# Attention output projection of a hybrid decoder step: when the shares of the merge are loaded and accumulated

## The chip, the cores and the metric

The kernel runs on one core of one Trainium2 chip. The metric is device time in microseconds (us) of one execution. Five engines work beside each other, each on its own list of instructions in a fixed order: TensorE (PE, with its weight loads as PEld), VectorE (DVE), ScalarE (ACT), GpSimd (POOL) and SyncE (SP). SP issues nearly all loads; POOL issues the transfers that add to what lies in SBUF ("accumulating" below). All transfers are carried by the core's 16 DMA engines.

## The reference, cut to what matters

One layer of a decoder for 1024 prompt tokens and 8 sample tokens (1032 columns, `TT`), width 1024. Three branches read the same normalised input, and their outputs are gated, summed and projected:

```python
y_c = jnp.einsum('bhlm,bmhd->blhd', probs, mem_v).reshape(bsz, seq, ATTN_DIM) @ w_attn_o
g_a, g_b, g_c = jnp.split(jax.nn.sigmoid(gates), N_BRANCHES, axis=-1)
merged = g_a * y_a + g_b * y_b + g_c * y_c
return merged @ w_merge_o, (sc_new, ssm_conv_new, ssm_new)
```

A SwiGLU block and a final norm follow. All is float32 in and out. A product is made of three passes over operands that are split into a high and a low part (high x high, high x low, low x high).

## The kernel before, in words

Activations lie as eight tiles of 128 partitions x 1032 columns, features on the partitions. The columns are handled in two halves of 516 (`HS`); the eight sample tokens are the last eight columns of the second half.

The first two branches are ready early: `g_a*y_a` lies in DRAM as `mg_d[m]`, `g_b*y_b` as `yg_d[m]`, for the eight output tiles m. These two are called the *shares* of tile m. The third branch is made last: the attention output of the prompt is loaded back as `raw8[0..7]` (line 1837), the sample columns are put into it by `s_back` from a PSUM tile (line 1752: four copies on DVE, four on ACT), and `y_c` is the product of `raw8` with `w_attn_o`.

That product is done by a Strassen-like scheme with seven half-size products on 2x2 blocks. The blocks of the activations and their sums and differences are called *forms*: B11, B21, T1, nT2, T3, B22, T4, four pieces each. A form is split into high and low by ACT (line 444) and DVE (line 446). T1 is `b12 - b11` (line 1887) and nT2 is `T1 - b22` (line 1891). Both need the second half of the columns, so their last eight columns need `s_back`. In the kernel before, T1 and nT2 are formed in two pieces each: 508 columns, and then the eight sample columns.

The output tiles are made in four pairs, m = 0, 2, 4, 6, called pair one to four below. Each pair runs `strassen` (line 298 is its matmul, and the names ao0, ao2, ao4, ao6 belong to the pairs): weights `ao{m}r` are loaded in two blocks into a ring of three buffers (line 279), their sums `sa` and `sb` are made on DVE (`sb` ends at line 331), and all are split (lines 285 and 286; `S`, `T`, `A`, `D` name the splits). Within it, `mid` calls `fetch` ahead of the product with T3: it loads the pair's two gates `gt_d[16+m]`, `gt_d[17+m]` (line 1956) and, from pair three on, the shares.

`shares(ms)` loads `yg_d[m]` into a new tile `merged[m]` on SP (line 1930), placed behind the last weight block issued so far (`issue_after(last_raw[0])`), and then has POOL accumulate `mg_d[m]` onto it (line 1931), which waits until the load has landed. Pair two's shares are called for ahead of its `strassen`. For pair one the tile is first filled with the gated product itself, and POOL then accumulates `yg_d` and `mg_d` onto tile 0 and 1 (line 1982, four transfers).

After a pair's product, DVE multiplies with the gates (lines 1970, 1971, 1975) and, for pairs two to four, adds onto `merged` (1973, 1974, 1977). Lines 432 and 434 are subtractions that end the pair's outputs and release PSUM.

All eight merged tiles are split (`mgs0`..`mgs7`, lines 180 and 181) and multiplied with `w_merge_o` (blocks `wm..`, line 170 and 171 for their split, line 2050 for the matmuls), in the order 0 to 7 of the inner index k.

The program's order is only a wish. The order on each engine is worked out ahead of the run by a planner, which takes, engine by engine, what is ready by its own estimate of durations, the earlier written first. `tc.issue_after(x)` adds one rule: the instructions in the block stand behind `x` on the queue of `x`. During the run each engine goes through its list strictly in order and waits where an input is late, whatever stands behind.

Of the kernel before, what the change touches and what calls it, by code (L numbers as in the profile page):

```python
# [12 lines left out]
ALU = mybir.AluOpType  # L13
# [4 lines left out]
P = 128  # L18
D = 1024
T = 1024  # L20
NS = 8
TT = T + NS
NCH = 3
CW = TT // NCH
HT = TT // 2
HC = HT // 2
KD = D // P
# [16 lines left out]
def tile_kernel(ctx: ExitStack, tc, a, o):  # L44
    nc = tc.nc
    V, S, G, PE, SY = nc.vector, nc.scalar, nc.gpsimd, nc.tensor, nc.sync

    def f32(t):
        return t.bitcast(F32)
# [24 lines left out]
    def act_tile(part, name, dt=F32R, shape=(P, TT)):  # L74
        return ap_.tile(list(shape), dt, tag=part, name=name)
# [101 lines left out]
    def split_act(src, name):  # L177
        hi = act_tile("ah", name + "h")
        lo = act_tile("al", name + "l")
        S.copy(hi, src)  # L180
        V.tensor_sub(lo, src, f32(hi))
        return hi, lo
# [74 lines left out]
    HS = [slice(0, HT), slice(HT, TT)]  # L257
# [17 lines left out]
    last_raw = [None]  # L275
# [167 lines left out]
    def split_to(hi, lo, src, behind=None):  # L443
        S.copy(hi, src)
        with nullcontext() if behind is None else tc.issue_after(behind):
            V.tensor_sub(lo, src, f32(hi))
# [6 lines left out]
    gt_d = dram("gt_d", [24, P, TT])  # L453
    mg_d = dram("mg_d", [KD, P, TT])
    yr_d = dram("yr_d", [KD, P, TT])
    yg_d = dram("yg_d", [KD, P, TT])
# [34 lines left out]
    with tc.tile_pool(name="p0", bufs=1) as p0, tc.tile_pool(name="pop", bufs=1, space=PSUM) as pop:  # L491
# [23 lines left out]
        ps = sm_ps("ps_mix")  # L515
# [6 lines left out]
        for key, src, n in (  # L522
# [13 lines left out]
            while done < n:  # L536
                b, off = divmod(at, P)
                m = min(n - done, P - off)
# [1093 lines left out]

    raw8, aforms = [], {}

    def aform(f, kt, src, c=slice(0, HT)):
        if kt % 2 == 0 and c.start == 0:
            mk = afx.get(f) or (lambda part, nm: act_tile(part, nm, shape=(P, 2, HT)))
            pair = [mk(part, f"a{f}{kt}{part}") for part in ("ah", "al")]
            aforms.setdefault(f, []).extend(tuple(t[:, i, :] for t in pair) for i in range(2))
        split_to(*(t[:, c] for t in aforms[f][kt]), src)  # L1640

    afx = {}
    if True:
# [100 lines left out]
        def s_back():  # L1744
            t = ev_tile("osr", (NS, D))
            SY.dma_start(t, os_d)
            ps = sm_ps("psob")
            for i in range(8):
                PE.transpose(ps[:, i * NS : (i + 1) * NS], t[:, i * P : (i + 1) * P], ident[:NS, :NS])
            for kt in range(KD):  # L1750
                cp_ = V.tensor_copy if kt < 4 else S.copy
                cp_(raw8[kt][:, T:TT], ps[:, kt * NS : (kt + 1) * NS])

        heads = {}
        slot = [None]
# [125 lines left out]
        one = lambda n: fxo.tile([P, TT], F32, tag="one", bufs=1, name=n)  # L1881
        begun = []
        ahead_of_last.append(lambda: begun.extend(st_begin(wa[0], wa[1], "ao0", lambda n: one(n)[:, :1024])))
        for c in (slice(0, T - HT), slice(T - HT, HT)):
            for kt in range(4):
                b11, b12 = (raw8[kt][:, h][:, c] for h in HS)
                V.tensor_sub(b11, b12, b11)
                aform("T1", kt, b11, c)
            for kt in range(4):
                t1, b22 = (raw8[kt + 4 * i][:, HS[i]][:, c] for i in range(2))  # L1890
                V.tensor_sub(t1, t1, b22)
                aform("nT2", kt, t1, c)
        run_next(outs)
        owed.pop()()

# [22 lines left out]
    merged = []  # L1918
# [4 lines left out]
        V.tensor_add(sa[:, 512:], sa[:, :512], raw1[:, :512])  # L1923
        return sa, st_split(sa, f"{nm}S")

    def shares(ms):
        for m in ms:
            merged.append(big(f"mg{m}"))
            with tc.issue_after(last_raw[0]):
                SY.dma_start(merged[m], yg_d[m])  # L1930
            G.dma_start(merged[m], mg_d[m], accum_op=ALU.add)

    second = []

    def last_forms_and_second():
        last_aforms()
# [4 lines left out]
    for m in range(0, KD, 2):  # L1941
        gts = []
        if m == 0:
            oo = oos[0]
        elif m == 2:
            oo = oos[1] + [ev_tile("ao21")[:, :TT]]
            begun = second
            shares(range(2, 4))
        else:
            oo = [ev_tile(f"ao{m}{i}")[:, :TT] for i in range(2)]  # L1950
            begun = None

        def fetch():
            for i in range(2):
                gts.append((ev_tile if i else one)(f"gt3{m + i}")[:, :TT])
                SY.dma_start(gts[i], gt_d[16 + m + i])
            if m > 2:
                shares(range(m, m + 2))

        pa = strassen(  # L1960
            wa[m], wa[m + 1], aforms, f"ao{m}", ev_sums, lambda: tuple(t[:, c] for t in oo for c in HS),
            begun=begun, mid=fetch, hook=None if m else form3,
            after_t3=None if m else last_forms_and_second, head=heads_[m // 2] if m < 4 else None,
        )
        if m == 2:
            accs.clear()
            accs.extend((ta, tb, tc_))
        c1, c0 = HS[1], HS[0]
        to = [big(f"mg{i}") for i in range(2)] if m == 0 else oo
        V.tensor_mul(to[0], oo[0], gts[0])  # L1970
        V.tensor_mul(to[1][:, c1], oo[1][:, c1], gts[1][:, c1])
        if m:
            V.tensor_add(merged[m], merged[m], to[0])
            V.tensor_add(merged[m + 1][:, c1], merged[m + 1][:, c1], to[1][:, c1])
        V.scalar_tensor_tensor(to[1][:, c0], pa, -1.0, gts[1][:, c0], op0=ALU.mult, op1=ALU.mult)
        if m:
            V.tensor_add(merged[m + 1][:, c0], merged[m + 1][:, c0], to[1][:, c0])
        else:
            merged += to
            for src in (yg_d, mg_d):  # L1980
                for i in range(2):
                    G.dma_start(merged[i], src[i], accum_op=ALU.add)
    fxo_stack.close()
    aux_stack = ExitStack()
    auxp = aux_stack.enter_context(tc.tile_pool(name="aux", bufs=3))
# [1 line left out]
    def aux(name):  # L1987
        return auxp.tile([P, TT], F32, tag="aux", name=name)

    mg = [split_act(merged[m], f"mgs{m}") for m in range(KD)]  # L1990

    x2 = [None] * KD
    rfs = [None, None]
# [32 lines left out]
    def form_first(kt):  # L2026
        form("B11", kt, normed(kt, 0))
# [4 lines left out]
    for half in range(2):  # L2032
        sq = ev_tile(f"sq{half}")
        for m in range(KD):
            xt = aux(f"xT{half}{m}")
            SY.dma_start(xt[:, :HT], xT_d[m][:, HS[half]])
            wh, wl = weights(wblock(a["w_merge_o"][0], m * P), f"wm{half}{m}")
            if half == 0:
                x2[m] = big(f"x2_{m}")
            t = x2[m][:, HS[half]]  # L2040

            def merge_part(out, ns):
                for k, (ah, al) in enumerate(mg):
                    if k in (0, 3, 6) and ns[0] == 0:
                        tick()
                    ks = slice(k * P, (k + 1) * P)
                    for i, (wt, x) in enumerate(((wh, ah), (wh, al), (wl, ah))):
                        for n, po in zip(ns, out):
                            lo, hi = HALF[n]
                            PE.matmul(  # L2050
                                po, wt[:, ks], x[:, half * HT + lo : half * HT + hi],
                                start=(k == 0 and i == 0), stop=(k == KD - 1 and i == 2),
                            )

            if half == 1 and m == KD - 1:

                for n, (lo, hi) in enumerate(HALF):
                    ps = sm_ps(f"pm{half}{m}{n}")[:, : hi - lo]
                    merge_part([ps], (n,))
                    V.tensor_tensor(t[:, lo:hi], ps, xt[:, lo:hi], op=ALU.add)  # L2060
            else:
                ps = next_ps(f"pm{half}{m}")
                merge_part([hv(ps)[:, lo:hi] for lo, hi in HALF], (0, 1))
                V.tensor_tensor(t, hv(ps), xt[:, :HT], op=ALU.add)  # L2064
            if m == 0:
                S.activation(sq[:, :HT], t, AF.Square)
            else:
                S.activation(xt[:, :HT], t, AF.Square)
                V.tensor_add(sq[:, :HT], sq[:, :HT], xt[:, :HT])
            S.dma_start(x2_d[m][:, HS[half]], t)  # L2070
        if half == 0:
            pend.extend([None, None] + [lambda sq=sq: norm_half(0, sq)] + [None])
            for kt in range(4):
                pend.extend([lambda kt=kt: form_first(kt), None, lambda kt=kt: form_second(kt), None])
        else:
            flush()
            norm_half(1, sq)
# [26 lines left out]
    for kt in range(4):  # L2104
        b12, b11 = normed(kt, 1), x2[kt][:, HS[0]]
# [3 lines left out]
    for kt in range(4):  # L2109
        t1, b22 = x2[kt][:, HS[0]], normed(kt + 4, 1)  # L2110
        V.tensor_sub(t1, t1, b22)
        form("nT2", kt, t1)
    for kt in range(4):
        b12, b22 = x2[kt][:, HS[1]], x2[kt + 4][:, HS[1]]
# [119 lines left out]
    for part, js in enumerate(([0], [9, 10])):  # L2234
# [9 lines left out]
        for m in range(KD):  # L2244
            if not part:
                x2[m] = big(f"x3_{m}")
            for half in range(2):
                ps = next_ps(f"pd{part}{m}{half}")
                for k, (ah, al) in enumerate(hl):
                    ks = slice(k * cols + m * P % cols, k * cols + m * P % cols + P)  # L2250
# [4 lines left out]
                t = x2[m][:, HS[half]]  # L2255
# [127 lines left out]
    for n3, (c0, c1, tiles) in enumerate(  # L2383
# [3 lines left out]
        for ms in ((0, 1), (2, 3, 4), (5, 6, 7)) if n3 == 0 else ((0, 1, 2), (3, 4, 5), (6, 7)):  # L2387
# [53 lines left out]
```

## Time and profile before

| | |
|---|---|
| median of 3 runs | 2442.67 us (2442.17 to 2443.28) |
| profiled execution, its own time | 2437.72 us |
| its span, first to last instruction | 2436.0 us |
| PE busy | 2392.2 us, 98% of the span |
| DVE busy | 1646.8 us, 68% |
| ACT busy | 1113.5 us, 46% |
| POOL busy | 114.6 us, 5% |
| mean granted TensorE clock | 0.997 |
| moved by DMA | 407.90 MB, mean 167 GB/s |
| queue of SP | 336.44 MB, 44.6% of the 16 engines' span |
| queue of POOL | 5.28 MB, 1.1% |

The attention projection lies between about 1552 us and 1652 us of the span; the merge begins at 1652.10 us. A row of the timeline gives start, duration, engine, line, operation, output tile <- inputs and count; in brackets, how long the engine sat idle just before and what ended that. A row of the waits gives who waited for whom, the total in us, how many times, and the longest. A row of the windows gives a stretch, its length, the busy time of each engine with the number of instructions, the granted clock, the share of the DMA engines and GB/s. Buffer numbers are left out of tile names: `mg` is any of the merged tiles, `ao4r` either weight block of pair three.

### The profile page before, as it was taken

To read this page: it belongs to the slowest core of one execution; us is meant where nothing else is said; L and a number is where in the kernel's file an instruction comes from. 1 tells how busy PE (TensorE), PEld (TensorE's weight loads), DVE (VectorE), ACT (ScalarE), POOL (GpSimd) and SP (SyncE) were. 2 spreads that over 40 slices of the span, in tenths; PEclk is the share of its full clock that TensorE was granted. 3 is DMA by queue.
4 is the path that set the end of the run, shared out by engine and by line. 5 is a ranking of instruction groups with operands and counts; after the bars stand their busy time and mean duration, and the time that the engine had idled before them with its cause. 6 is when DMAs were issued, how large, how long until landed. Compare 5 with 4: busy or idle time off the path is not lost.

```text
span 2436.0 us, 45644 instructions
## 1 busy us (share of the span) xinstructions
PE 2392.2 (98%) x18860; PEld 2284.5 (94%) x18860; DVE 1646.8 (68%) x2689; ACT 1113.5 (46%) x1792; POOL 114.6 (5%) x173
## 2 busy tenths in 40 slices
PE   8999999999999999999999999889999999999998
PEld 6999999999999999888888987889999999999998
DVE  6744677777777775568687764765777655567965
ACT  6643555455454543656555442333553333343423
POOL 0000000000000000212211000010000000000000
PEclk9999999999999999999999999999999999999999
DMA  6444423444444345668787797495455333354622
GB/s 204 135 154 160 137 87 109 136 140 131 125 150 122 115 118 187 215 222 281 247 294 219 272 320 263 142 244 186 141 179 168 101 109 100 97 175 156 192 86 81
DMA packets 356678, 407.90 MB, mean 167 GB/s; under 512 B 15230, under 2 KB 276462, under 8 KB 356463
## 3 DMA queue, kind: packets, MB, share of 16 engines
q1 hardware_dynamic: 331894, 336.44, 44.6%
q10 hardware_dynamic: 23137, 63.26, 6.8%
q0 software_dynamic: 1440, 5.28, 1.1%
q8 instruction: 148, 2.42, 0.4%
q14 instruction: 59, 0.48, 0.1%
HBM read 288.81 MB, written 116.35 MB: 166 GB/s over the span
## 4 chain that ended last, share of the span: by engine, by line
PE 87%; DMA 5%; DVE 4%; issue 2%; ACT 2%; SPq 0%; POOL 0%; DVEq 0%; ACTq 0%; POOLq 0%
PE po L221 7%; PE pm L2050 4%; PE ps_q L221 3%; PE py L1114 1%; PE pss L1127 1%; PE ps_z L221 1%; PE po L1106 1%; DMA in<-yb_d 1%; PE G16m L298 1%; PE d00m L298 1%; PE G22m L298 1%; PE Z2m L298 1%; PE Z14m L298 1%; PE Z6m L298 1%; PE Z8m L298 1%
## 5 line engine op out<-in xcount | busy, mean ns | idle before, releaser
L1058 ACT ACTIVATE r<-r,acum 128x128 f32<-128x128 f32 x256 | 79.3, 391 | 2.8 <-DMA r<-ac_d 1.9
L847 DVE SCALAR_TENSOR_TENSOR ax<-u,prm,ax 128x1024 f32<-128x1024 f32 x44 | 56.4, 1282 | 0.0
L999 ACT ACTIVATE st<-st,es 128x128 f32<-128x128 f32 x128 | 41.3, 392 | 18.2 <-DMA st<-in_state_ssm_dram 15.1
L1091 POOL TENSOR_TENSOR xdd<-xdt,decst 128x512 f32<-128x512 f32 x32 | 35.2, 1101 | 285.3 <-DVE xdt L1087 279.4
L1085 DVE TENSOR_TENSOR r<-r,cbm 128x1024 f32<-128x1024 f32 x32 | 39.2, 1224 | 4.3 <-ACT r L1060 2.4
L1001 DVE SCALAR_TENSOR_TENSOR st<-sr,dts,st 128x128 f32<-128x128 f32 x128 | 40.8, 353 | 0.4
L1110 DVE TENSOR_TENSOR y<-po,ea 128x512 f32<-128x512 f32 x28 | 19.3, 690 | 31.2 <-PE po L1106 31.2
L1005 DVE SCALAR_TENSOR_TENSOR sr<-st,sr 128x128 f32<-128x128 f32 x128 | 35.9, 291 | 1.1
L1127 PE MATMUL pss<-xdd,bT 128*128 128x512 f32 x64 | 34.4, 619 | 2.2 <-ACT bT L1084 1.4
L1114 PE MATMUL py<-r,xdt 128*64 128x128 f32 x512 | 35.0, 279 | 0.0
L1060 ACT ACTIVATE r<-r 128x1024 f32<-128x1024 f32 x32 | 33.8, 1057 | 0.7
L1140 POOL TENSOR_TENSOR s<-s,cdec 128x512 f32<-128x512 f32 x28 | 33.1, 1183 | 0.6 <-DVE s L1133 0.4
L2064 DVE TENSOR_TENSOR x<-pm,xT 128x516 f32<-128x516 f32 x15 | 10.4, 695 | 32.0 <-PE pm L2050 32.0
L1114 PEld LDWEIGHTS py<-r,xdt 128*64 128x64 f32 x512 | 27.3, 136 | 4.4 <-issue 1.0
L1106 PE MATMUL po<-bc,s 128*128 128x128 f32 x224 | 29.5, 275 | 0.0
L1106 PEld LDWEIGHTS po<-bc,s 128*128 128x128 f32 x224 | 28.0, 191 | 1.0
L1694 ACT ACTIVATE pr<-psa,mx 128x256 f32<-128x256 f32 x32 | 14.9, 471 | 30.5 <-DVE mx L1692 26.6
L850 DVE SCALAR_TENSOR_TENSOR ax<-u,prm,ax 128x1032 f32<-128x1032 f32 x22 | 28.4, 1291 | 0.0
L844 ACT ACTIVATE ax<-u,prm 128x1024 f32<-128x1024 f32 x22 | 27.4, 1246 | 1.2 <-ACT u L926 0.4
L1087 DVE TENSOR_TENSOR xdt<-xp,dtT 128x512 f32<-128x512 f32 x32 | 21.9, 685 | 8.8 <-PE xp L1080 8.7
L1084 ACT COPY bT<-bp 128x128 f32<-128x128 f32 x32 | 8.4, 262 | 39.3 <-DVE cbm L1082 39.2
L1682 DVE SCALAR_TENSOR_TENSOR kc<-kc,qb 128x256 f32<-128x256 f32 x64 | 23.8, 421 | 3.3 <-DMA qb<-qs_d 3.3
(9293 smaller groups left out, 9067.4 us busy)
## 6 DMA issues: line engine op xcount, KB each, us to landing
r<-ac_d SPq DMA_DIRECT2D x32, 512.0 KB
gt_d<-G ACTq DMA_DIRECT2D x24, 516.0 KB
gt<-gt_d SPq DMA_DIRECT2D x24, 516.0 KB
xs_d<-ax ACTq DMA_DIRECT2D x22, 516.0 KB
zs<-zs_d SPq DMA_DIRECT2D x16, 516.0 KB
yb_d<-x SPq DMA_DIRECT2D x16, 516.0 KB
in<-yb_d SPq DMA_DIRECT2D x16, 516.0 KB
st<-in_state_ssm_dram SPq DMA_DIRECT2D x32, 256.0 KB
```

The costliest lines, as they stand in the source:

```text
L221: PE.matmul(po, wt[:, ks], xc, start=(k == 0 and i == 0), stop=(k == nk - 1 and i == 2))
L298: PE.matmul(po, wt[:, ks], xc, start=(start and kt == 0 and i == 0), stop=(kt == 3 and i == 2), skip_group_check=True,)
L847: V.scalar_tensor_tensor(acc[:, :T], u[:, j : j + T], w[j], acc[:, :T], op0=ALU.mult, op1=ALU.add)
L999: S.activation(st[:, i], st[:, i], AF.Copy, scale=es[:, g * 4 + i, b : b + 1])
L1001: V.scalar_tensor_tensor(st[:, i], rb, dts[:, g * 4 + i, b : b + 1], st[:, i], op0=ALU.mult, op1=ALU.add)
L1005: V.scalar_tensor_tensor(rb, st[:, i], 1.0, rc, op0=ALU.mult, op1=ALU.mult, accum_out=ys[:, g * 4 + i, b : b + 1],)
L1058: S.activation(r[:, j, :], r[:, j, :], AF.Relu, scale=-1.0, bias=acum[:, c, h : h + 1])
L1085: V.tensor_tensor(r, r, bc(cbm.unsqueeze(1), [P, HPG, P]), op=ALU.mult)
L1106: PE.matmul(po[:, t * P : (t + 1) * P], state["s"][:, t * P : (t + 1) * P], bcg[1][:, cs], start=True, stop=True,)
L1114: PE.matmul(py[hp : hp + 64, (h // 2) * P : (h // 2 + 1) * P], xdt[:, h * 64 : (h + 1) * 64], r[:, (h % 2) * 4 + h // 2, :], start=True, s ...
L1127: PE.matmul(pss, bT, xdd, start=True, stop=True)
L2050: PE.matmul(po, wt[:, ks], x[:, half * HT + lo : half * HT + hi], start=(k == 0 and i == 0), stop=(k == KD - 1 and i == 2),)
```

## The change

Five edits, all around this stage:

1. T1 and nT2 are formed in whole pieces of 516 columns: 8 differences and 8 splits in place of 16 and 16.
2. The copies of the sample columns into `raw8` are all on ACT.
3. The shares of pairs three and four are loaded behind the second gate of the same pair (`got[0]`) instead of behind the last weight block. Pair two's are as before.
4. Pair one's four accumulating transfers are written after pair three's `strassen` and placed behind the last accumulating transfer of pair three (`added[0]`) on POOL's queue.
5. The merge takes its inner index in the order 2, 3, 4, 5, 0, 1, 6, 7, and the merged tiles are split in that order.

```diff
-    def aform(f, kt, src, c=slice(0, HT)):
-        if kt % 2 == 0 and c.start == 0:
+    def aform(f, kt, src):
+        if kt % 2 == 0:
...
-        split_to(*(t[:, c] for t in aforms[f][kt]), src)
+        split_to(*aforms[f][kt], src)
...
-                cp_ = V.tensor_copy if kt < 4 else S.copy
-                cp_(raw8[kt][:, T:TT], ps[:, kt * NS : (kt + 1) * NS])
+                S.copy(raw8[kt][:, T:TT], ps[:, kt * NS : (kt + 1) * NS])
...
-        for c in (slice(0, T - HT), slice(T - HT, HT)):
-            for kt in range(4):
-                b11, b12 = (raw8[kt][:, h][:, c] for h in HS)
-                V.tensor_sub(b11, b12, b11)
-                aform("T1", kt, b11, c)
-            for kt in range(4):
-                t1, b22 = (raw8[kt + 4 * i][:, HS[i]][:, c] for i in range(2))
-                V.tensor_sub(t1, t1, b22)
-                aform("nT2", kt, t1, c)
+        for kt in range(4):
+            b11, b12 = (raw8[kt][:, c] for c in HS)
+            V.tensor_sub(b11, b12, b11)
+            aform("T1", kt, b11)
+        for kt in range(4):
+            t1, b22 = raw8[kt][:, HS[0]], raw8[kt + 4][:, HS[1]]
+            V.tensor_sub(t1, t1, b22)
+            aform("nT2", kt, t1)
...
-    def shares(ms):
+    def shares(ms, behind):
         for m in ms:
             merged.append(big(f"mg{m}"))
-            with tc.issue_after(last_raw[0]):
+            with tc.issue_after(behind):
                 SY.dma_start(merged[m], yg_d[m])
-            G.dma_start(merged[m], mg_d[m], accum_op=ALU.add)
+            added[0] = G.dma_start(merged[m], mg_d[m], accum_op=ALU.add).ins
...
-            shares(range(2, 4))
+            shares(range(2, 4), last_raw[0])
...
-                SY.dma_start(gts[i], gt_d[16 + m + i])
+                got[0] = SY.dma_start(gts[i], gt_d[16 + m + i]).ins
             if m > 2:
-                shares(range(m, m + 2))
+                shares(range(m, m + 2), got[0])
...
+        if m == 4:
+            for src in (yg_d, mg_d):
+                for i in range(2):
+                    with tc.issue_after(added[0]):
+                        G.dma_start(merged[i], src[i], accum_op=ALU.add)
...
             merged += to
-            for src in (yg_d, mg_d):
-                for i in range(2):
-                    G.dma_start(merged[i], src[i], accum_op=ALU.add)
...
-    mg = [split_act(merged[m], f"mgs{m}") for m in range(KD)]
+    mg = [(m, split_act(merged[m], f"mgs{m}")) for m in (2, 3, 4, 5, 0, 1, 6, 7)]
...
-                for k, (ah, al) in enumerate(mg):
+                for k, (kt, (ah, al)) in enumerate(mg):
...
-                    ks = slice(k * P, (k + 1) * P)
+                    ks = slice(kt * P, (kt + 1) * P)
```

More of the change, by code (lines that the diff above doesn't have):

```diff
@@ L1924, in sums_of @@
         return sa, st_split(sa, f"{nm}S")
-    def shares(ms):
+    def shares(ms, behind):
         for m in ms:
             merged.append(big(f"mg{m}"))
-            with tc.issue_after(last_raw[0]):
+            with tc.issue_after(behind):
                 SY.dma_start(merged[m], yg_d[m])
-            G.dma_start(merged[m], mg_d[m], accum_op=ALU.add)
-    second = []
+            added[0] = G.dma_start(merged[m], mg_d[m], accum_op=ALU.add).ins
+    added = [None]
+    second, got = [], [None]
     def last_forms_and_second():
```

## The prediction

> **What bounds the kernel now.** The page comes first: which engine carries the chain that ended last.
>
> ```profile
> span 2436.0 us, 45644 instructions
> PE 87%; DMA 5%; DVE 4%; issue 2%; ACT 2%; SPq 0%; POOL 0%; DVEq 0%; ACTq 0%; POOLq 0%
> ```
>
> PE carries 87%, so an edit pays only where PE stands still for it. The chain of waits between 1590 and 1660 us, the waits from 1480 to 1680 us, and windows of 5 us say where it does.
>
> ```profile
> 1583.75 9.26 issue
> ...
> 1594.66 16.08 DMA mg<-mg_d
> ```
> ```profile
> DVE mg L1974 <- DMA mg<-mg_d: 8.0, 1, 8.0
> ...
> ACT ao4Ah L285 <- DMA ao4r<-in_w_attn_o_dram: 5.5, 1, 5.5
> ...
> PE ao2m L298 <- ACT ao L383: 3.9, 1, 3.9
> ...
> PE ao0m L298 <- ACT aT10ah L444: 1.3, 1, 1.3
> ```
> ```profile
> 1550.00:1555.00 5.00, 5.00 (x43) 4.80 (x41) 5.00 (x13) 1.78 (x3) 0.00 (x0) 1.00 0.51 139
> ...
> 1595.00:1600.00 5.00, 4.01 (x21) 4.01 (x22) 2.61 (x3) 0.94 (x2) 1.56 (x2) 0.68 1.09 322
> ...
> 1615.00:1620.00 5.00, 5.00 (x35) 5.00 (x34) 3.68 (x5) 1.54 (x2) 0.00 (x0) 0.77 1.03 268
> ```
>
> Two stalls stand out. In pair two PE waits 3.9 us for a PSUM copy on ACT that stands behind `ao4Ah`, which waits for a weight block. At pair three DVE waits 8.0 us for an accumulating transfer that took 16.08 us. Afterwards the clock is 0.68 and 0.77 for 5 us. The timeline of POOL shows why that transfer was late.
>
> ```profile
> 1582.73 1.01 POOL L1982 DMA_DIRECT2D mg<-yg_d  x1 [274.03 <-DVE mg L1970]
> 1593.03 0.87 POOL L1982 DMA_DIRECT2D mg<-mg_d  x1 [9.28 <-DMA mg<-yg_d]
> ...
> 1594.12 2.44 POOL L1931 DMA_DIRECT2D mg<-mg_d  x2
> ...
> 1626.06 0.85 POOL L1931 DMA_DIRECT2D mg<-mg_d  x1 [18.03 <-DMA mg<-yg_d]
> 1627.76 0.86 POOL L1931 DMA_DIRECT2D mg<-mg_d  x1 [0.85 <-DMA mg<-yg_d]
> ```
>
> Pair two's two transfers (1594.12) stand behind pair one's, for whose first POOL waits 9.28 us. DVE and PE, each by its timeline:
>
> ```profile
> 1602.11 0.69 DVE L434 TENSOR_TENSOR ao<-ao,ao2m 128x516 f32<-128x516 f32 x1
> 1610.83 0.70 DVE L1974 TENSOR_TENSOR mg<-mg,ao 128x516 f32<-128x516 f32 x1 [8.03 <-DMA mg<-mg_d]
> ...
> 1612.58 1.22 DVE L286 TENSOR_TENSOR ao4Sl<-ao4sa,ao4Sh 128x1024 fp32r<-128x1024 f32 x1
> ...
> 1616.80 0.69 DVE L331 SCALAR_TENSOR_TENSOR ao4sb<-ao4sa,ao4r 128x512 f32<-128x512 f32 x1
> ...
> 1628.10 0.69 DVE L1974 TENSOR_TENSOR mg<-mg,ao 128x516 f32<-128x516 f32 x1
> ...
> 1631.38 1.22 DVE L286 TENSOR_TENSOR ao6Sl<-ao6sa,ao6Sh 128x1024 fp32r<-128x1024 f32 x1
> ```
> ```profile
> 1581.40 0.51 PE L298 MATMUL ao2m<-aT10ah,ao2Sh 128*128 128x256 f32 x2 [3.12 <-ACT ao2Sh L285]
> ...
> 1613.86 0.80 PE L298 MATMUL ao4m<-aT10ah,ao4Sl 128*128 128x256 f32 x2 [5.62 <-DVE ao4Sl L286]
> ...
> 1635.47 0.40 PE L298 MATMUL ao6m<-aT10ah,ao6Sl 128*128 128x256 f32 x2
> ...
> 1656.40 0.41 PE L2050 MATMUL pm<-mgs6h,wm00h 128*128 128x256 f32 x2
> ```
>
> DVE's order is fixed, so `ao4Sl`, which PE needs, stood behind the late add of line 1974: 5.62 us lost. From 1613.86 to the merge PE hardly waits.
>
> **The change, part by part.** *T1 and nT2 whole, sample copies on ACT.* The rows, first and last of each kind on DVE:
>
> ```profile
> 1547.12 0.39 DVE L1752 COPY at<-psob 128x8 f32<-128x8 f32 x4 [0.82 <-PE psob L1749]
> ...
> 1550.41 1.88 DVE L1891 TENSOR_TENSOR at<-at,at 128x508 f32<-128x508 f32 x3
> ...
> 1554.60 0.40 DVE L1887 TENSOR_TENSOR at<-at 128x8 f32<-128x8 f32 x4
> ...
> 1556.83 0.23 DVE L446 TENSOR_TENSOR aT10al<-at,aT10ah 128x8 fp32r<-128x8 f32 x2
> ```
> ```profile
> L1887 DVE TENSOR_TENSOR at<-at x8: 165/426/690, 1507.3 to 1554.8; 128x508 f32<-128x508 f32 x4, 128x8 f32<-128x8 f32 x4
> ```
>
> Sixteen eight-column pieces go: two groups of four differences at 0.40, four groups of two splits at 0.23, together 1.7 us of DVE; with the four copies, 0.39, it is 2.1. But the four wide T1 differences, which began at 1507.3 under other work, now need the sample columns and move past 1547: 4 x 0.63 (1.88 for three) = 2.5. DVE is busy without a gap there (5.00 of 5 us in the first window), so the sum is +0.4, or -0.4 if the 0.82 wait for `psob` goes too. I take +0.3; the upper end is +1.3, the wait that PE has at ao0 now, a second time, for pieces that come late. ACT trades eight short casts for four copies: no cost, since DVE paces it.
>
> *Pair one's accumulations leave POOL's queue at pair two, and pair three's loads leave SP's.* SP, from its timeline:
>
> ```profile
> 1582.53 0.86 SPq L1930 DMA_DIRECT2D mg<-yg_d  x2
> ...
> 1588.84 4.36 SPq L1930 DMA_DIRECT2D mg<-yg_d  x2
> ...
> 1617.56 0.38 SPq L279 DMA_DIRECT2D ao6r<-in_w_attn_o_dram  x1
> 1617.99 1.59 SPq L1956 DMA_DIRECT2D gt<-gt_d  x1
> 1619.62 0.91 SPq L1930 DMA_DIRECT2D mg<-yg_d  x2
> ```
> ```profile
> DMA to landing us min/median/max: 7.9/10.2/16.1
> ```
>
> First stall: `ao4r` shared the engines with pair one's first accumulation, 0.528 MB. At 268 GB/s (the last window) that is 2.0 us, so the 3.9 us become 1.9, and no cold clock follows (the 3.12 us wait at 1581.40 was followed by full speed): 5 x (1 - 0.68) = 1.6 more. Gain 3.6; the ends are 0 and 5.5.
>
> Second stall: pair two's loads are issued at 1582.53. In the pair issued at 1619.62 the two accumulations followed after 6.4 and 8.1 us; so here 1589.0 and 1590.7. With the median landing of 10.2 us the second is there at 1600.9. Line 1974 then starts at 1600.9, and `ao4Sl` ends 2.97 us after that (1612.58 + 1.22 - 1610.83): 1603.9. PE used to stop at 1613.86 - 5.62 = 1608.24, now 3.6 earlier, 1604.6. No stall is left: 5.62, and 5 x (1 - 0.77) = 1.15 of clock. With 16.1 us to landing nothing of it is gained. Both together: 10.4 us, between 0 and 12.3.
>
> *Pair three's shares behind its gates.* This adds a wait. The second gate stands behind `ao6r`, whose buffer comes free when line 331 ends, 6.66 us after line 1974 began (1616.80 + 0.69 - 1610.83): now 1607.6. Exactly this train, weight block, gate, two loads, two accumulations, ran in before for pair four: from 1617.56 to the second accumulation 10.2 us, to its landing 7.9 more (the minimum, since nothing else accumulated). Of the 18.1, the gate's issue took 1.59 where SP's loads otherwise take about 0.4, in a stretch in which the DMA share was 1.03; less backlog takes off 1.3. So 16.8 us: landing at 1624.5. The ends are 14.8 (first share 6.4, landing 7.9, 0.5 to issue) and 20.4 (10.2 + 10.2). Line 1974 of this pair would come at 1628.10 - 10.4 = 1617.7, so DVE stands for almost 7 us. Behind it are lines 434 and 1970 and `ao6Sl`. I let the planner put 434 ahead, as it did in pair two, its one late pair; then `ao6Sl` ends 2.97 after the landing, 1627.5. PE is there at 1635.47 - 10.4 = 1625.1: 2.4 us lost, under the 3.12 that kept the clock. Gain left: 8.0.
>
> *Pair four's shares behind its gates, pair one's accumulations behind pair three's.* The same train starts again at the weight block behind line 331 of ao6.
>
> ```profile
> 1636.73 0.69 DVE L331 SCALAR_TENSOR_TENSOR ao6sb<-ao6sa,ao6r 128x512 f32<-128x512 f32 x1
> ...
> 1648.06 0.70 DVE L1974 TENSOR_TENSOR mg<-mg,ao 128x516 f32<-128x516 f32 x1
> ```
> ```profile
> 1653.73 1.06 ACT L180 CAST mgs6h<-mg 128x1032 fp32r<-128x1032 f32 x1 [0.61 <-DVE mg L1973]
> ```
>
> It ended 4.82 after `ao6Sl` (1637.42 against 1632.60): 1632.3, so the train lands at 1649.2. From line 1974 to the end of `mgs6h` it was 6.7 us, without 0.7 of idle time and with 434 ahead 5.4: 1654.6. PE wants `mgs6h` at 1656.40 - 8.0 = 1648.4 and stands for 6.2 us; the cold clock then costs about 1.4 (1.15 and 1.6 above). So PE is 1.8 - 1.4 = 0.4 us ahead of before. Pair one's four accumulations are issued in between and fill time in which POOL did nothing; the new k order lets the merge run on six tiles meanwhile, which I cost at nothing because PE's wait for `mgs6h` covers it.
>
> **Sum:** +0.3 - 3.6 - 6.8 + 2.4 + 6.2 + 1.4 = -0.1, made against the profiled execution's own 2437.72 (its span and 1.72 around it), which would become 2437.6. It ran 4.95 below the median of the runs, 2442.67; against that median: 2442.6.
>
> **The rivals.**
> *The new waits are covered (faster).* If the train lands within the 10.6 us that line 1974 has in before (1617.49 to 1628.10), or the planner puts `ao6Sl` and the merge's splits ahead of line 1974, neither stall appears: -10.4 + 0.3 = -10.1, 2432.6. For it: in pair two the planner did put other work ahead. Against: 6.4 + 7.9 is already 14.3. The Trainium skill ("DMA: Bandwidth & Descriptors", section "Anatomy of one DMA") gives a transfer issued by GpSimd as about 2.0 us + bytes / 436 GB/s, an estimate of 3.2 us for 0.528 MB; by that rule two in series land in time and this rival holds. The trace disagrees: 7.9 at least.
>
> *Pair four's shares land as late as pair two's did (slower).* One mechanism: pair one's four accumulations are now issued just ahead of pair four's two and share the 16 engines with them and their loads. With 16.1 us to landing instead of 7.9, the merge starts 8.2 us later: 2450.8. It decides for "slower" from about 5.5 us on. For it: the same neighbourhood gave 16.08 in before. Against: by the times above they are issued from 1617 on and have some 30 us. The Trainium skill (same page, "Queues, rings and completion order") has each engine go round between the queues it has work for, so moving them on POOL's queue saves none of their bytes; that speaks for this rival.
>
> *The change does not do what it says:* pair two's transfers land late all the same, at 16.1. Then 3.6 is the whole gain, and the two trains follow from a late start: line 331 at 1617.5 as before, and PE loses 5.5 + 1.4 at the first (it is there 3.6 us earlier, at 1631.9, and `ao6Sl` ends at 1637.4) and 4.8 + 1.4 at the second, so the end moves by -3.6 + 13.1 + 0.3 = +9.8, 2452.5.
>
> **How the numbers follow.** About 0.2% (4.9 us) is what a measurement of this kernel tells from no change. Gain handed back, likeliest: 0.43, with its own range 2438 to 2447 from the ends of the trains (two times -2.0 to +3.6, damped by PE's slack). Covered: 0.29. Late again: 0.22. No effect: 0.06. A few of the likeliest fall over each edge: faster 0.32, same 0.39, slower 0.29. The range runs from the covered case to the late one, 2432 to 2451.
>
> **What would show it.** Right: POOL issues pair two's accumulations near 1589, no 8 us on line 1974 of pair two, PE's 5.62 gone; then idle time of 5 to 8 us on DVE at line 1974 in pairs three and four, and a PE gap at the merge's `mgs6h` near 6 us. Wrong: no idle time at these two lines (covered), landings over 13 us in pair four (late), or PE gaps around 1556, where T1 comes later than I say.

## The result, and the profile after

| kernel | median us | runs | ratio to before, 95% interval |
|---|---|---|---|
| before, on the same chip | 2441.97 | 10 | |
| after | 2447.61 | 10 | 1.0028 [1.0018, 1.0038] |
| after, once more (`after_again`, below) | 2450.09 | 5 | 1.0039 [1.0025, 1.0053] |

The change makes the kernel slower by about 6 to 10 us: the medians differ by 5.6 us, and by 10.4 us in `after_again`, which ran beside a before of 2439.73. The forecast was no change. The two profiled executions differ by 2445.3 - 2436.0 = 9.3 us of span. Lines of the changed file stand lower than in before: 1885 and 1889 are the T1 and nT2 differences, 1928 and 1929 the shares' loads and accumulations, 1969 pair one's accumulations, 1975, 1976 and 1980 the gate products, 1978, 1979 and 1982 the adds into `merged`, 2052 the merge's products. In the kernels of the experiments the same lines stand a few lines lower.

The page after: the span, and the shares of the chain that ended last.

```profile
span 2445.3 us, 45621 instructions
PE 86%; DMA 6%; DVE 5%; ACT 2%; issue 1%; SPq 0%; POOL 0%; DVEq 0%; ACTq 0%; POOLq 0%
```

PE still carries it, and DMA and DVE have one point more each. The waits of the stage (1480 to 1680 us), as in before: who waits for whom, us in total, times, longest.

```profile
DVE mg L1979 <- DMA mg<-mg_d: 13.1, 2, 8.6
...
PE pm L2052 <- ACT mgs6h L180: 7.4, 1, 7.4
...
DVE ao4sa L401 <- DMA ao4r<-in_w_attn_o_dram: 5.6, 1, 5.6
...
PE ao0m L298 <- DVE yr L1548: 4.1, 1, 4.1
...
PE ao2m L298 <- DVE ao L432: 3.9, 1, 3.9
```

Of PE's old waits, 3.9 us for a copy and 5.62 for `ao4Sl`, the first has fallen to 1.17 and the second is gone. Three stand in their place: 4.1 at `ao0`, 3.9 behind line 432 in pair two, 7.4 at the merge. DVE's one wait of 8.0 us for an accumulation has become two, 13.1 together. The timeline of POOL:

```profile
1589.34 1.01 POOL L1929 DMA_DIRECT2D mg<-mg_d  x1 [280.27 <-ACT ao2Dh L285]
1591.12 0.87 POOL L1929 DMA_DIRECT2D mg<-mg_d  x1 [0.76 <-DVE ao2Dl L286]
1618.93 0.86 POOL L1929 DMA_DIRECT2D mg<-mg_d  x1 [26.94 <-DVE ao4Dl L286]
1620.22 0.86 POOL L1929 DMA_DIRECT2D mg<-mg_d  x1 [0.42 <-issue]
...
1646.52 0.86 POOL L1929 DMA_DIRECT2D mg<-mg_d  x1 [11.40 <-DMA mg<-yg_d]
1648.99 0.86 POOL L1929 DMA_DIRECT2D mg<-mg_d  x1 [1.62 <-ACT wm01h L170]
```

Pair two's accumulations now go out at 1589 and 1591, four to five us earlier than in before, with no other transfer ahead of them on POOL's queue; pairs three's and four's start at 1619 and 1647, each behind its own loads. Such a chain of weight block, gate, loads and accumulations, each issued behind the one before, is called a *train* below, as in the prediction. DVE's timeline shows what each reaches:

```profile
1601.39 0.69 DVE L401 TENSOR_TENSOR ao4sa<-ao4r 128x512 f32<-128x512 f32 x1 [5.59 <-DMA ao4r<-in_w_attn_o_dram]
...
1602.73 0.69 DVE L432 TENSOR_TENSOR ao<-ao,ao2m 128x516 f32<-128x516 f32 x1
...
1604.66 0.69 DVE L1979 TENSOR_TENSOR mg<-mg,ao 128x516 f32<-128x516 f32 x1
...
1610.81 0.68 DVE L331 SCALAR_TENSOR_TENSOR ao4sb<-ao4sa,ao4r 128x512 f32<-128x512 f32 x1
...
1629.04 0.70 DVE L1979 TENSOR_TENSOR mg<-mg,ao 128x516 f32<-128x516 f32 x1 [4.46 <-DMA mg<-mg_d]
...
1636.88 0.69 DVE L331 SCALAR_TENSOR_TENSOR ao6sb<-ao6sa,ao6r 128x512 f32<-128x512 f32 x1
...
1656.73 0.70 DVE L1979 TENSOR_TENSOR mg<-mg,ao 128x516 f32<-128x516 f32 x1 [8.63 <-DMA mg<-mg_d]
```

Pair two's add (1604.66) waits for nothing any more. But two places ahead of line 432 stands the first sum of pair three's weights, which waits 5.59 us for its weight block (0.87 us in before, where the block was there at about 1597.5); line 432 empties the PSUM that PE wants. The chain of waits has the block, and the two accumulations (8.73 and 7.64 us) that end in the two late adds:

```profile
1587.84 13.43 DMA ao4r<-in_w_attn_o_dram
...
1620.22 8.73 DMA mg<-mg_d
...
1648.99 7.64 DMA mg<-mg_d
```

PE's three stops, from its timeline, and the windows of 5 us around the last two (length, then busy time of PE, PEld, DVE, ACT and POOL, granted clock, DMA share, GB/s):

```profile
1559.14 0.77 PE L298 MATMUL ao0m<-aB210ah,ao0Ah 128*128 128x256 f32 x2 [4.06 <-DVE yr L1548]
...
1603.47 0.80 PE L298 MATMUL ao2m<-aT40ah,ao2Dh 128*128 128x256 f32 x2 [3.87 <-DVE ao L432]
...
1662.71 0.80 PE L2052 MATMUL pm<-mgs6h,wm00h 128*128 128x256 f32 x2 [7.43 <-ACT mgs6h L180]
```
```profile
1600.00:1605.00 5.00, 1.53 (x7) 1.53 (x8) 3.54 (x6) 1.05 (x1) 0.00 (x0) 0.66 0.24 70
1605.00:1610.00 5.00, 5.00 (x30) 5.00 (x30) 4.88 (x6) 0.00 (x0) 0.00 (x0) 0.65 0.34 106
...
1655.00:1660.00 5.00, 0.28 (x3) 0.07 (x1) 3.24 (x4) 0.00 (x0) 0.00 (x0) 0.97 0.14 27
1660.00:1665.00 5.00, 1.88 (x7) 1.58 (x7) 5.00 (x6) 2.10 (x2) 0.00 (x0) 0.50 0.91 271
1665.00:1670.00 5.00, 4.89 (x23) 4.89 (x24) 2.95 (x4) 1.69 (x3) 0.00 (x0) 0.51 0.39 100
```

After each stop PE runs on at half its clock for about 5 us, after the last for 7. The 0.66 and 0.65 are means of windows in which the clock changed: after the stop in pair two the granted clock is 0.50 until about 1608.5 and 1.00 from there, and PE's rows of two products, 0.43 us apart until then, are 0.24 apart behind it.

To compare profiles whose earlier parts differ by a few us, the experiments go by the **stage**: from PE's first `ao0` product to SP's issue of `wm13r` in the merge. It takes 136.99 us in before and 146.75 in after (+9.8); the rest of the span is 2299.0 and 2298.6. Over all the profiled executions here that rest lies between 2298.6 and 2303.5, so medians that are a few us apart say less than the stages. A stage measured a second time came out 0.03 and 0.33 us apart (after; `four_early`). Points in it, as us from its start:

| kernel | B21 of `ao0` | pair two's T4 | `ao4Sl` | `ao6Sl` | merge | `mgs6h` | stage |
|---|---|---|---|---|---|---|---|
| before | 4.35 | 49.92 | 61.87 | 83.48 | 100.11 | 104.41 | 136.99 |
| after | 7.07 | 51.40 | 59.96 | 80.73 | 98.75 | 110.64 | 146.75 |
| `t1_whole` | 7.07 | 51.03 | 62.98 | 85.78 | 102.41 | 106.71 | 139.29 |
| `shares_only` | 4.35 | 49.80 | 57.64 | 78.99 | 96.99 | 108.64 | 144.75 |
| `one_late` | 4.35 | 49.56 | 58.12 | 78.09 | 94.73 | 99.03 | 131.60 |
| `four_early` | 7.07 | 50.19 | 58.33 | 81.25 | 99.55 | 103.85 | 137.28 |
| `three_early` | 7.11 | 51.97 | 60.71 | 80.69 | 97.32 | 107.08 | 143.79 |
| `one_left_out` | 7.07 | 51.67 | 60.25 | 81.53 | 99.55 | 110.16 | 146.73 |
| `two_left_out` | 7.07 | 45.53 | 51.81 | 74.06 | 92.36 | 103.04 | 138.60 |
| `two_plain` | 7.06 | 48.59 | 54.87 | 77.74 | 96.03 | 108.84 | 145.07 |
| `sums_late` | 4.35 | 44.41 | 57.98 | 77.17 | 94.73 | 99.01 | 132.10 |
| `late_two_out` | 4.34 | 45.53 | 51.70 | 72.49 | 89.12 | 93.42 | 126.07 |

(Each is PE's first product on what the column names.)

### The profile page after: what moved, and what is told of

Read it like the earlier page. It is cut to its first block, busy times and chain, and to the rows that moved or that the text cites. A ratio compares the mean times of both kernels' runs of the same rounds, so it can differ in the third digit from the quotient of the medians.

```text
span 2445.3 us, 45621 instructions
## 1 busy us (share of the span) xinstructions
PE 2395.5 (98%) x18860; PEld 2287.7 (94%) x18860; DVE 1645.2 (67%) x2669; ACT 1112.0 (45%) x1788; POOL 115.6 (5%) x173
## 4 chain that ended last, share of the span: by engine, by line
PE 86%; DMA 6%; DVE 5%; ACT 2%; issue 1%; SPq 0%; POOL 0%; DVEq 0%; ACTq 0%; POOLq 0%
PE po L221 7%; PE pm L2052 4%; PE ps_q L221 3%; PE pd L2256 1%; PE py L1114 1%; PE pss L1127 1%; PE ps_z L221 1%; PE po L1106 1%; PE G16m L298 1%; PE d00m L298 1%; PE Z2m L298 1%; PE Z14m L298 1%; PE X18m L298 1%; PE Z6m L298 1%; PE Z8m L298 1%
## 5 line engine op out<-in xcount | busy, mean ns | idle before, releaser
L2066 DVE TENSOR_TENSOR x<-pm,xT 128x516 f32<-128x516 f32 x15 | 10.4, 695 | 34.2 <-PE pm L2052 34.2
```

## Experiments: the parts alone

**T1 alone.** Edit: the kernel before with the first part of the diff (`aform` without columns, the copies on ACT, the two loops over whole pieces), nothing else.

> Edits 1 and 2 alone: T1 and nT2 in whole pieces, all sample copies on ACT; shares, accumulations and k order as in before. Theory (the late shares cost most, T1 little): +1 to +3 us against before; PE's wait at the B21 product of ao0 is about 4 us as in the changed kernel (1.34 in before), because line 1548, which empties the PSUM tile that product needs, stands behind the T1 and nT2 work on DVE. Rival (the T1 edit is the whole loss): +6 us or more. Rival (the small pieces saved pay for the wide ones): 0.

Measured: 2440.13 us, ratio 1.0008 [0.9999, 1.0017]; stage +2.3. PE's timeline:

```profile
1561.29 0.48 PE L298 MATMUL ao0m<-aB210ah,ao0Ah 128*128 128x256 f32 x2 [4.06 <-DVE yr L1548]
```

The same 4.06 us as in after, against 1.34 in before. Line 1548 empties the PSUM bank that this product wants. In before DVE did it between the small pieces, at 1555.50; now it comes behind all of T1 and nT2, at 1558.30 in after:

```profile
1555.50 0.70 DVE L1548 TENSOR_TENSOR yr<-po,yr 128x516 f32<-128x516 f32 x1
```
```profile
1556.34 0.47 PE L298 MATMUL ao0m<-aB210ah,ao0Ah 128*128 128x256 f32 x2 [1.34 <-ACT aT10ah L444]
```
```profile
1558.30 1.29 DVE L1548 TENSOR_TENSOR yr<-po,yr 128x516 f32<-128x516 f32 x2
```

(The first two are before's, the third is after's.) In before too the product starts 0.14 us behind the end of line 1548, though its row names a cast on ACT. The part costs 2.3 us of stage; in time its interval still reaches no change.

**The shares alone.** Edit: the kernel after with the T1 part put back as before.

> Edits 3, 4 and 5 alone: T1 in two pieces and the sample copies as in before. Theory: +4 to +7 us against before; the first product with ao2Sh starts where it did in before, but DVE still waits at the add of pair three (4 us or more) and of pair four (about 8 us), and PE waits about 7 us for mgs6h. Rival (the T1 edit is the whole loss): 0 or faster than before.

Measured: 2445.72, ratio 1.0029 [1.0019, 1.0040]; stage +7.8. With T1's 2.3 that is 10.1 against 9.8 for the whole: the parts add. Both late trains are there without T1 (waits of the stage):

```profile
DVE mg L1981 <- DMA mg<-mg_d: 13.4, 2, 8.4
...
PE pm L2054 <- ACT mgs6h L180: 7.2, 1, 7.2
```

**Pair one's accumulations and the k order alone.** Edit, to the kernel before:

```diff
-            for src in (yg_d, mg_d):
-                for i in range(2):
-                    G.dma_start(merged[i], src[i], accum_op=ALU.add)
+        if m == 4:
+            for src in (yg_d, mg_d):
+                for i in range(2):
+                    with tc.issue_after(added[0]):
+                        G.dma_start(merged[i], src[i], accum_op=ALU.add)
```
with the merge's new k order; all shares stay behind the last weight block.

> Before with edits 4 and 5 alone: pair one's accumulations behind pair three's, merge's k order; all shares are loaded as in before, T1 as in before. Theory: pair two's accumulations land near 1601, DVE's 8 us wait and PE's 5.6 us go, and no train comes late: -4 to -9 us against before. Rival (pair two's accumulations starve the second weight block of pair three, as the changed kernel's 13.4 us load suggests): PE waits some 4 us behind line 401 instead, and no more than -3 us is left. Rival (the engines' total work is what counts, the order of the transfers does not): 0.

Measured: 2431.97, ratio 0.9972 [0.9961, 0.9983], stage -5.4: faster than both kernels, by 6.6 us against before. No add and no merge product waits for an accumulation here. PE's waits ahead of pair two's T3 (1.3 and 3.1 us) are before's; behind them one stop is left, with the weight block again, which takes 13.32 us (waits of the stage):

```profile
DVE ao4sa L401 <- DMA ao4r<-in_w_attn_o_dram: 5.4, 1, 5.4
...
PE ao2m L298 <- DVE ao L432: 3.7, 1, 3.7
```

**One train each.** Edit, to the kernel after: `four_early` puts pair four's shares back behind the last weight block and leaves pair three's behind its gates; `three_early` is the reverse.

```diff
-                shares(range(m, m + 2), got[0])
+                shares(range(m, m + 2), got[0] if m == 4 else last_raw[0])
```

> The changed kernel, but pair four's shares are loaded behind pair four's last weight block, as in before; pair three's stay behind the gates. Theory: the last train goes, the 8.6 us wait of DVE at pair four's add and PE's 7.4 us wait for mgs6h go with its cold clock: 7 to 10 us under the changed kernel, so between -3 and +1 against before. Rival (the T1 edit, or pair two's accumulations beside the weight loads, make the loss): no more than 3 us under the changed kernel, +4 against before.

> The whole change, but pair three's shares are issued behind the last weight block, as in the kernel before; pair four's stay behind pair four's gates. Theory (two trains that add up: pair four's delays the merge's `mgs6h`, pair three's delays pair four's own start): pair three's wait at its first add (4.46 in the profile after) goes, pair four's train stays at 17 to 19 us from `wm01r`'s gate transfer to the landing, a wait of PE for `mgs6h` of 4 to 8 us stays. Stage from the first `ao0` product to the issue of `wm13r`: 140 to 144 us (146.75 after, 136.99 before); time 2 to 5 us below the changed kernel, so +2 to +5 over the kernel before. Rival (pair three's train does nothing by itself, its wait is covered): no more than 1 us below the changed kernel, +6 or more over before.

> The same kernel as `four_early` once more, since its profiled execution (span 2436.1, stage 137.28) lay at the low end of its times (2437.84 to 2445.61, median 2441.91). Theory (pair three's train costs about 3.4 us of stage over `one_late` with T1 in whole pieces, and the median reads high): stage 136 to 139 us, median within 2 us of the kernel before. Rival (part of its executions have a longer stage, which the one profile missed): a stage of 140 us or more, or again a median 3 us or more above the kernel before.

Measured: `four_early` 2441.91, ratio 1.0019 [1.0010, 1.0027], stage 137.28; again, 2443.22, 1.0007 [0.9996, 1.0017], stage 137.61; `three_early` 2443.82, 1.0019 [1.0009, 1.0028], stage 143.79. In `three_early` the add of pair three does not wait, that of pair four does:

```profile
DVE mg L1979 <- DMA mg<-mg_d: 7.9, 1, 7.9
...
PE pm L2052 <- ACT mgs6h L180: 5.3, 1, 5.3
```

By stages the parts add up within 0.5 us: `one_late` 131.6, T1 2.3, pair three's train 3.4 (`four_early`), pair four's 9.5 more (after), which is 9.9 without pair three's (`three_early`). So pair four's train is the dear one: it ends in PE's stop at the merge, while pair three's lateness costs PE only 0.65 us at `ao6Sl` in after. In `four_early` pair four's loads go out together with pair three's, whose add then waits 6.61 us instead of 4.46, so its 3.4 us are not pair three's alone. `four_again` shows the same stage a second time. The medians of this kernel lie 3 us above before, with a stage 0.3 to 0.6 longer; the time expected of `four_early`, -3 to +1 us against before, and that of `four_again`, within 2 us, were missed. That stays open within intervals that reach from -1 to +6.6 us.

**Pair one's accumulations as a burden on pair four.** Edit, to the kernel after: the loop under `if m == 4` is taken out, so pair one's shares are missing from the sum.

> The whole change without pair one's four accumulations (its merged tiles 0 and 1 then hold only the gated projection; that part of the sum is left out). Theory (pair four's train is long by its own three steps, weight block, gates, loads and accumulations): the train falls from 19.0 to about 17 us, `mgs6h` comes 1 to 3 us earlier against the stage's start, time 1 to 3 us under the changed kernel. Rival (pair four's transfers are slow because pair one's four transfers of 0.5 MB run beside them): train 14 us or less, PE's wait ahead of the merge's last tiles under 3 us, time 5 us or more under the changed kernel.

Measured: 2449.46, ratio 1.0041 [1.0026, 1.0055], stage 146.73, the same as after. Pair four's train, from SP's issue of `wm01r` (1639.60) to the landing (1657.31), is 17.7 us instead of 19.0 (1637.63 to 1656.63), but its start is 0.8 later in the stage, and `mgs6h` comes only 0.5 earlier. The rival of the prediction by which these four transfers delay pair four by 8.2 us is out: they lengthen the train by 1.3 us, and the stage does not show even that.

## Experiments: the weight block beside the accumulations

The second `ao4r` block takes 13.43 us in after. Four kernels ask why, and what it is worth; three of them leave a part of the sum out.

**Without pair two's accumulations.** Edit, to the kernel after:

```diff
-            added[0] = G.dma_start(merged[m], mg_d[m], accum_op=ALU.add).ins
+            if m > 3:
+                added[0] = G.dma_start(merged[m], mg_d[m], accum_op=ALU.add).ins
```

> The whole change without the accumulation of `mg_d` into pair two's merged tiles 2 and 3 (that part of the sum is left out). Theory (the second `ao4r` weight block takes 13.43 us in the changed kernel because pair two's two accumulations run beside it): the block lands in 5 to 9 us, the wait of 5.6 us of the sum `ao4sa` and PE's 3.9 us behind line 432 go, the clock of 1600 to 1610 stays above 0.9; everything behind it 3 to 5 us earlier against the stage's start, time 2 to 5 us under the changed kernel. Rival (the block is slow by itself or by the gates' loads): it still takes over 11 us and PE's wait stays over 3 us.

Measured: 2442.11, ratio 1.0012 [1.0003, 1.0020], stage 138.60, 8.2 under after, more than the 3 to 5 expected; by the ratios the time is 4 to 7 us under the two measurements of after. The chain of waits has the block at 8.45 us, and PE runs through the window in which it had stood:

```profile
1588.73 8.45 DMA ao4r<-in_w_attn_o_dram
```
```profile
1600.00:1605.00 5.00, 5.00 (x45) 5.00 (x44) 5.00 (x7) 0.17 (x1) 0.00 (x0) 1.00 0.31 94
```

So the accumulations slow the block, and the block stops PE. The 8.2 us are mostly the stop of 3.87, some 2.5 of half clock behind it (5 us at 0.50) and the copy's 1.17. PE's wait for `mgs6h` stays, at 6.2 us: two separate causes.

**Adding, or only bytes?** Edit, to the kernel after: the same two transfers, same queue and place, `accum_op` left out for pair two, so that they overwrite the other share.

> The whole change, with pair two's two transfers of `mg_d` kept on the same queue, at the same place and of the same bytes, but as plain loads that overwrite instead of accumulations (pair two's merged tiles then lack the share of `yg_d`). Theory A (it is the adding that slows the weight block beside it): the second `ao4r` block, 13.43 us in the changed kernel and 8.45 without the two transfers, takes 8 to 10 us, PE's wait behind line 432 falls under 1 us, and the stage shortens towards 138.6. Theory B (it is the bytes alone: 1 MB more in the same window): the block stays over 12 us and PE's wait over 3 us.

Measured: 2445.39, ratio 1.0021 [1.0011, 1.0030], stage 145.07. The block takes 11.36 us, between the two theories: of the 4.98 us over 8.45, the bytes make 2.9 and the adding 2.1. PE's wait behind line 432 falls from 3.87 to 1.67, and the clock stays at 1.00 there; pair four's wait at the merge grows to 8.3 and eats most of it. The DMA queues of 1586 to 1604 us (packets, MB, share of 16 engines), after first, then `two_plain`:

```profile
q1 hardware_dynamic: 3629, 3.41, 58.4%
q0 software_dynamic: 288, 1.06, 29.7%
```
```profile
q1 hardware_dynamic: 3627, 3.40, 58.5%
q0 software_dynamic: 288, 1.06, 15.5%
```

The same 1.06 MB hold the engines for 29.7% of 18 us when they add, 5.3 us, and 15.5%, 2.8 us, when they don't: 198 against 380 GB/s. The loads' own bytes and share are the same. The Trainium skill ("DMA: Bandwidth & Descriptors", section "Queues, rings and completion order") states that an engine goes round between the queues that have work, packet by packet; by that rule a load waits longer where the other queue's packets hold the engines longer. The trace agrees, 13.43 and 11.36 against 8.45; the page has no price for adding.

**Without them in `one_late`.** The edit of `two_left_out`, made to `one_late`, where pair three's two plain loads run beside the block on its own queue.

> `one_late` (the kernel before with pair one's accumulations behind pair three's and the new k order) without the accumulation of `mg_d` into pair two's merged tiles 2 and 3 (that part of the sum is left out). There pair three's two plain loads of `yg_d` and a gate still run beside the second `ao4r` block. Theory (the accumulations are what holds the block up): block under 9 us, no wait of PE behind line 432, stage 122 to 127 us (131.60 in `one_late`). Rival (any 1 MB beside the block does it): block over 11 us, PE's wait over 3 us, stage within 2 us of 131.6.

Measured: 2428.23, ratio 0.9946 [0.9931, 0.9961], stage 126.07. The wait that was 5.4 us:

```profile
DVE ao4sa L401 <- DMA ao4r<-in_w_attn_o_dram: 0.5, 1, 0.5
```

The block, issued at 1589.52, is there by 1597.8, 8.3 us against 13.32 in `one_late`: 1 MB of plain loads behind it on its own queue does not hold it up. What these accumulations still cost `one_late` is 5.5 us of stage.

**The sum issued later.** Edit, to `one_late`: `ao4sa`'s first sum issued behind pair two's last subtraction, so that it no longer stands ahead of line 432 (the diff shows only the sum; `late` is that subtraction).

```diff
-                V.tensor_add(sa[:, :512], raw2[:, :512], raw2[:, 512:])
+                with nullcontext() if late is None else tc.issue_after(late):
+                    V.tensor_add(sa[:, :512], raw2[:, :512], raw2[:, 512:])
```

> The kernel before with pair one's accumulations behind pair three's and the merge's new k order alone (`one_late`), and in addition DVE's first sum of pair three's weights, `ao4sa`, issued behind pair two's last subtraction (line 434 before). Theory (the sum waits 5.4 us for the second `ao4r` block and stands ahead of the adds that empty pair two's PSUM, so that PE waits 3.7 us and then runs at a granted clock of 0.66): PE's wait falls under 1 us, the granted clock of 1600 to 1610 stays above 0.9, stage 127 to 130 us (131.60 in `one_late`), time 2 to 5 us under `one_late`, 8 to 11 under the kernel before. Rival (the sum is itself on the path: its tiles are wanted at once by PE, so the wait comes back at pair three's third or fifth product): stage within 1 us of 131.6, same time as `one_late`.

Measured: 2434.04, ratio 0.9975 [0.9965, 0.9986], stage 132.10: the rival holds, nothing is gained over `one_late`. The wait moved (waits of the stage):

```profile
DVE mg L1984 <- DMA mg<-mg_d: 3.6, 1, 3.6
...
PE ao4m L298 <- DVE ao L1985: 2.9, 1, 2.9
```

Line 432's work is done in time, but DVE then stands 3.6 us at pair two's add, and with it line 1985, which empties the next bank.

**The changed kernel again**, beside `two_plain`, `late_two_out` and `four_again`.

> The changed kernel once more, on the same chip as the three others. Theory: stage 145 to 148 us, ratio to the kernel before 1.002 to 1.004, waits of PE of 3.5 to 4.2 us behind line 432 and of 6 to 8 us for `mgs6h`.

Measured: 2450.09, ratio 1.0039 [1.0025, 1.0053], stage 146.72. PE's waits are 5.2 behind line 432 and 8.2 for `mgs6h`, 1.0 and 0.2 over the ranges expected; the block takes 13.54.

## Why the prediction was wrong, point by point

The mechanism was forecast in part: two trains, weight block, gate, loads, accumulations, give a gain back at pairs three and four. But the gain they were to give back was not there. The sum of -0.1 became +9.8 of stage. Step by step (us in the two profiles; the stages begin within 0.1 of each other):

| step | forecast | measured |
|---|---|---|
| T1 and nT2 whole | +0.3, at most +1.3 | +2.3 (`t1_whole`) |
| pair two's accumulations issued | 1589.0, 1590.7 | 1589.34, 1591.12 |
| line 1974 (now 1979) of pair two | 1600.9 | 1604.66 |
| line 331 of `ao4` ends | 1607.6 | 1611.5 |
| pair three's train | 16.8 | 17.4 (1611.56 to 1628.95) |
| `ao6Sl` ends, after the landing | 2.97 | 3.8 |
| PE's stop at `ao6Sl` | 2.4 | 0.65, PE being late itself |
| pair four's train | 16.8 | 19.0 |
| end of `mgs6h` | 1654.6 | 1662.66 |
| clock behind the merge's stop | 1.4 | about 3.4 |

**The step that failed is the second stall.** "No stall is left" priced pair two's add by its own accumulation alone, and that came true: the add does not wait. But the accumulations, set free, run beside the second `ao4r` block, which then takes 13.43 us, and the sum that waits for it stands in DVE's order ahead of line 432. PE stops for 3.87 us and runs on at half its clock for 5 us. The term of -6.8 came to about -0.9: 5.62 us of stop and 1.7 of clock went (3.4 us at 0.50 in before), 3.87 of stop and 2.5 of clock came. The prediction had charged just this neighbourhood once, to pair one's accumulation in the first stall, and dropped the charge when the transfers changed places. Without the two accumulations (`two_left_out`) PE starts `ao4Sl` 51.81 us into the stage; the forecast's 1604.6 is 52.6 into before's. The price of the omission is at most the 8.2 us of stage of `two_left_out`, where pair two's add has no accumulation to wait for at all.

**T1 was mis-sized.** DVE's work did grow by little, and the first window did stay full. Counting busy time missed the order: line 1548, on which PE waits, went from the middle of the pieces to behind them. My upper end, one more wait of 1.3, was too low, and it took that wait for one on the pieces, as its row names ACT, where line 1548 ended just ahead of the product.

**Pair four's train was mis-sized** by 2.2 us, and what follows it by 0.6. In after its second accumulation is issued 2.5 us behind the first, in pair three 1.3; in `one_left_out` 1.4, with a train of 17.7. The cold clock was sized at 1.4 from windows at 0.68 and 0.77; it came as 1660 to 1670 at 0.50 and 0.51, 6.77 us of PE's work at half speed, so 3.4. The two old windows were themselves means: at the second, half-us windows give 0.50 until 1617, which is 1.7 us and not 1.15.

From the late line 331 of `ao4` (+3.9) on, the trains' excess (0.6 and 2.2), the later `ao6Sl` (0.8) and the rest (0.6) make up the 8.1 us by which `mgs6h` is late. With 2.0 more of clock, and without the 0.3 for T1, which the sum had put on top of this chain, that is 9.8 of the 9.9 between -0.1 and +9.8.

**Right:** the first stall shrinks (1.17 us are left of 3.9, 1.9 were forecast), the issue times, no wait at pair two's add, idle time at the adds of pairs three and four (4.46 and 8.63, each just outside the 5 to 8 named), a stop at `mgs6h` (7.43 for 6.2). The planner put line 1979 ahead of 434, which takes 0.7, in both late pairs, not behind it as I had let it; that is most of the 0.8 and of the 0.6.

**The rivals.** "Covered" is out: both adds waited. The Trainium skill's formula on which it leaned ("DMA: Bandwidth & Descriptors", section "Anatomy of one DMA") gives an estimate of 3.2 us for a transfer that took 7.64 and 8.73. "Pair four late like pair two" named the right side, and its 2450.8 is nearer than mine, but not for its reason: pair four's accumulation landed in 7.64 us, not 16.1, and leaving pair one's out changed no stage. That 2447.6 lies inside the range up to 2451 is luck for the same reason, since this rival set that end. "The change does not do what it says" is out by the issue times.

## What to carry to other kernels

A transfer that is moved to an earlier place takes engine time from whatever loads there: list the loads in the new window, ask which of them an engine is already waiting for, and charge an accumulating transfer by the engine time that its queue's row shows, here twice that of a plain one. A load that is put behind an event becomes a train of issue, load and accumulation, here 17 to 20 us for 1 MB of shares: set that length against the slack of its consumer before moving it, above all where the consumer ends the stage. Of a change in several parts, each part is worth a run alone: here one part is worth -6.6 us and the others together lose more than that.

## What was not expected of the hardware

Accumulating transfers held the DMA engines twice as long per byte as plain ones of the same shape (198 and 380 GB/s), and 1 MB of plain loads queued behind a block on its own queue did not delay it (8.3 us; 8.45 without them), while the same bytes on the other queue did (11.36).

The Trainium skill ("TensorE: Matmul & The Clock Gate", Part 1) gives an idle window of about 3.4 us for the fall to half clock. By the length of the single stops the traces agree: 3.12 us in before kept 1.00, and 3.87 in after gave 0.50. By the moment of the fall they do not: PE's stop in after begins at 1599.60, and half-us windows give 1.00 until 1601.5 and 0.50 from 1602, some 2 us into it. So a stop need not last 3.4 us before the clock falls. In `sums_late` it fell without any stop of that length; PE's timeline and the window behind it:

```profile
1608.38 0.50 PE L298 MATMUL ao4m<-aB210ah,ao4Ah 128*128 128x256 f32 x2 [2.92 <-DVE ao L1985]
...
1610.14 0.66 PE L298 MATMUL ao4m<-aT10ah,ao4Sh 128*128 128x256 f32 x2 [0.55 <-ACT ao4Sh L285]
```
```profile
1610.00:1615.00 5.00, 4.86 (x28) 4.86 (x29) 3.17 (x4) 1.62 (x3) 0.00 (x0) 0.66 1.03 216
```

(0.66 is again a mean: 0.50 until 1613.5, then 1.00.) A stop of 2.92 us and a second, short one just behind it went ahead of the fall; what else it may depend on was not tried.
